# A two-pass matrix MLP with a guarded fallback: moving branch hints, splitting early outputs and shifting one ScalarE square

## Chip, cores, metric

One core of one Trainium2 chip. The metric is the device time of one execution in microseconds (us), as the median of several runs.

In the profiles PE is the tensor engine (PEld its weight loads), DVE is VectorE, ACT is ScalarE, POOL is GpSimd, and SP is the engine that here only issues DMAs. A q behind a name means the engine's sequencer, which runs the waits, jumps and DMA issues. A branch hint is an instruction (BRANCH_PREFETCH_HINT in the traces, 45 to 56 ns), put somewhere ahead of a branch, with which the program tells an engine which way the branch will probably go. Hit and miss are used here for what the traces show at the jump: on SP and DVE the next instruction started 0.45 to 0.54 us after the end of the jump (a hit) or 2.5 to 3.0 us after it (a miss); on PE the branch instruction took 0.4 us, and 3.7 us in the one run without a hint (e6).

## The reference

```python
def reference(x, w1, w2):            # x 16x256x512, w1 512x4096, w2 2048x512, all f32
    h = x @ w1
    gate, value = np.split(h, 2, axis=-1)
    h = np.maximum(gate, 0) * value
    return (h @ w2).astype(np.float32)
```

## The kernel before

The rows of x are worked in four sets of 1024. Each set has a first matmul phase (x by w1, then gate times value into `g`) and a second (g by w2). Both form a 2x2 block product from seven products P1 to P7 (a Strassen-like scheme) in f16. The kernel trusts that only for inputs of a usual size, so along the way it sums squares of x, w1 and w2. In the last set it judges the sums, and a branch at the end runs a slow general body if they don't fit:

```python
    with ExitStack() as fast:
        unfit = fast_way(fast, tc, x2, w1, w2, out2, flag)
    with tc.If(unfit > 0, label="general"):        # line 42 of the kernel
        with ExitStack() as general:
            general_way(general, tc, x2, w1, w2, out2)   # a long body on PE, DVE and SP
```

With the inputs used here the branch always jumps over the general body. The second matmul of a set works on four pairs of row blocks. What each product is followed by (cut):

```python
    class Pair:
        def __init__(self, s, g, t):
            self.end = s == NS - 1 and t == NB // 2 - 1     # only the very last pair: four pieces
        # P2: ScalarE evicts X to o[:,0,:256];  if end: send that piece
        # P3: VectorE evicts W to o[:,0,256:];  send (half or whole row block)
        # P7: VectorE evicts Y to o[:,1,256:];  if end: send that piece
        def P6(self):
            nc.scalar.activation(self.pu[:, 1], self.Y, COPY, scale=1 / GS)   # P7 accumulates into Y after this
            for _ in range(0 if self.s and self.t == 3 else 2 if self.s else 1):
                some_look()                                  # one square of weights, 128x1024, on ScalarE
        def P4(self):
            nc.scalar.activation(self.o[:, 1, :DO // 2], self.Y, COPY, scale=1 / GS)
            self.send(1, slice(0, DO // 2 if self.end else DO))
            if self.t < (2 if self.s else 3):
                some_look()

    ORDER = ("P1 0, P1 1, P2 0, P2 1, P1 2, P5 0, P2 2, P6 0, P3 0, P7 0, P5 1, P6 1, P3 1, P7 1, P4 0, P5 2, P4 1, "
             "P6 2, P3 2, P7 2, P1 3, P4 2, P5 3, P2 3, P6 3, P3 3, P7 3, P4 3")
```

This is the order of sets 1 and 2; sets 0 and 3 use variants of it, which also end with P4 of pair 3. The hints are traced in the last set, but no dependency holds them there. In the built program they come first on PE, DVE and SP, right behind two start-up instructions:

```python
            job(90, lambda: tc.mark_branch_hint_location("general", "LikelyTaken", [ENG.PE, ENG.DVE, ENG.SP]))
```

At the end of set 0, VectorE makes sums of the next set's x, which comes by transposing DMA. The trace has them in the order of the program (the sums from 83.03, the last pair's evictions behind them at 84.36 and 84.70):

```python
            if s == 0:
                sums = sums_of(xo)
                for u in (84, 90):                   # steps of the second matmul's stream
                    job(u, lambda sums=sums: next(sums))
            ...
            advance(stream, 112 - TAIL - 10, jobs)
            if s == 0:
                next(sums)
                next(sums)
```

## Time and profile before

| | before |
|---|---|
| time, median of 3 runs | 311.19 us (311.07 to 311.42) |
| span of the profiled run | 309.16 us, granted clock 0.999 |
| PE busy | 301.5 us, 98% |
| first gap-free PE stretch begins | 23.3 us |
| last ScalarE eviction ends | 304.96 us |
| from there to the end | 4.20 us |

The page's part 1 and part 4 (busy time with its share of the span, and the chain of work that ended last, by engine and by line) say what bounds the kernel:

```profile
PE 301.5 (98%) x1870; PEld 183.2 (59%) x1870; DVE 236.4 (76%) x378; ACT 177.0 (57%) x350; POOL 153.7 (50%) x186
...
PE 93%; DVE 2%; DMA 2%; issue 1%; SPq 0%; ACT 0%; DVEq 0%
PE Y L233 26%; PE X L233 17%; PE W L233 17%; PE Y L333 14%; PE X L333 9%; PE W L333 9%; DMA x_A<-in_x_dram 2%; DVE x_S L164 1%; PE X L448 1%; DVE g L308 1%; PE X L301 1%; PE W L301 1%; PE W L448 0%; PE Y L150 0%; DVE x_S L450 0%
```

PE is the chain (93% of it). I count any wait on PE after 23 us as lost time one for one, and so anything in the tail after PE has finished.

First, a wait on PE in sets 1 and 2. This is the chain in order of time, before, near 223 us (start, length, what, how many):

```profile
222.59 0.87 PE W L333 x8
223.46 0.04 issue
223.50 1.03 PE Y L333 x8
```

Eight matmuls normally take 0.87 us. The group at 223.50 takes 1.03 and comes 0.04 late: 0.20 us lost. The same stands at 150.48. ScalarE's timeline before (start, length, engine, line, operation, shapes) shows what PE waited for:

```profile
221.75 0.38 ACT L376 ACTIVATE o<-Y 128x256 f32<-128x256 f32 x1
222.03 1.05 ACT L179 ACTIVATE sq<-v_B 128x1024 f16<-128x1024 f16 x1
222.98 0.19 ACT L179 ACTIVATION_READ_ACCUMULATOR sq<-v_B 128x1 f32 x1
223.07 0.37 ACT L360 ACTIVATE pu<-Y 128x256 f32<-128x256 f32 x1
223.34 1.06 ACT L179 ACTIVATE sq<-v_T 128x1024 f16<-128x1024 f16 x1
```

The product at 223.50 accumulates into Y, which ScalarE must have read first (`pu<-Y`, 223.07 to 223.44). That read stood behind a square that began at 222.03: 1.04 us from start to start, with its accumulator read in between.

Second, the jump at the end. These are the instructions that the sequencers ran for line 42, the branch, before (engine, operation, count; durations min/median/max in ns; first and last start in us):

```profile
L42 SPq EVENT_SEMAPHORE  x8: 17/17/17, 305.9 to 307.5; - x8
...
L42 PEldq COMPARE_BRANCH  x1: 397/397/397, 303.4 to 303.4; - x1
L42 DVEq COMPARE_BRANCH  x1: 90/90/90, 303.7 to 303.7; - x1
L42 DVEq EVENT_SEMAPHORE  x1: 21/21/21, 304.3 to 304.3; - x1
...
L42 SPq COMPARE_BRANCH  x1: 73/73/73, 305.4 to 305.4; - x1
```

The first instruction after SP's jump starts at 305.9, 0.45 us after the jump ended. SP then waits for eight DMA semaphores, one after the other, until 307.5; the last transfer landed at 307.17. The last ScalarE eviction, from which the tail is counted, was:

```profile
304.58 0.38 ACT L376 ACTIVATE o<-Y 128x256 f32<-128x256 f32 x1 [2.24 <-PE Y L333]
```

The hints stood at the very start:

```profile
L670 SPq BRANCH_PREFETCH_HINT  x1: 56/56/56, 0.7 to 0.7; - x1
L670 DVEq BRANCH_PREFETCH_HINT  x1: 51/51/51, 0.8 to 0.8; - x1
L670 PEldq BRANCH_PREFETCH_HINT  x1: 50/50/50, 0.8 to 0.8; - x1
```

And SP's own waits from 300 us on (engine and line, what it waited for: us in total, times, longest):

```profile
SPq L42 <- SPq L42: 1.7, 3, 0.8
```

That is 1.7 us in three waits: one between the jump and the next instruction (0.45 us), two for landings.

### The profile page before, as it was taken

To read this page: it belongs to the slowest core of one execution; us is meant where nothing else is said; L and a number is where in the kernel's file an instruction comes from. 1 tells how busy PE (TensorE), PEld (TensorE's weight loads), DVE (VectorE), ACT (ScalarE), POOL (GpSimd) and SP (SyncE) were. 2 spreads that over 40 slices of the span, in tenths; PEclk is the share of its full clock that TensorE was granted. 3 is DMA by queue.
4 is the path that set the end of the run, shared out by engine and by line. 5 is a ranking of instruction groups with operands and counts; after the bars stand their busy time and mean duration, and the time that the engine had idled before them with its cause. 6 is when DMAs were issued, how large, how long until landed. Compare 5 with 4: busy or idle time off the path is not lost.

```text
span 309.2 us, 5211 instructions
## 1 busy us (share of the span) xinstructions
PE 301.5 (98%) x1870; PEld 183.2 (59%) x1870; DVE 236.4 (76%) x378; ACT 177.0 (57%) x350; POOL 153.7 (50%) x186
## 2 busy tenths in 40 slices
PE   7999999999999999999999999999999999999994
PEld 3844444588854444478864444458884444448883
DVE  1598888889678888887538888888536888888841
ACT  2588886445865555537855555546956555553231
POOL 2199999930048899500028889700006988700000
PEclk9999999999999999999999999999999999999999
DMA  7977696998594233001354400000325110000132
GB/s 236 355 230 251 176 232 87 196 214 149 164 303 101 69 70 68 2 0 47 127 184 105 119 0 4 0 0 15 122 103 171 37 34 1 0 3 0 70 136 72
DMA packets 37340, 32.87 MB, mean 106 GB/s; under 512 B 14400, under 2 KB 32320, under 8 KB 37184
## 3 DMA queue, kind: packets, MB, share of 16 engines
q1 hardware_dynamic: 31904, 25.70, 27.2%
q0 software_dynamic: 4352, 6.29, 11.8%
q10 hardware_dynamic: 1056, 0.52, 0.6%
q8 instruction: 15, 0.25, 0.3%
q14 instruction: 13, 0.11, 0.1%
HBM read 27.26 MB, written 12.58 MB: 129 GB/s over the span
## 4 chain that ended last, share of the span: by engine, by line
PE 93%; DVE 2%; DMA 2%; issue 1%; SPq 0%; ACT 0%; DVEq 0%
PE Y L233 26%; PE X L233 17%; PE W L233 17%; PE Y L333 14%; PE X L333 9%; PE W L333 9%; DMA x_A<-in_x_dram 2%; DVE x_S L164 1%; PE X L448 1%; DVE g L308 1%; PE X L301 1%; PE W L301 1%; PE W L448 0%; PE Y L150 0%; DVE x_S L450 0%
## 5 line engine op out<-in xcount | busy, mean ns | idle before, releaser
L233 PEld LDWEIGHTS <-w_T 128*128 128x128 f16 x496 | 48.5, 98 | 57.5 <-issue 1.0
L170 POOL TENSOR_TENSOR fold<-xh 128x1024 f32<-128x1024 f16 x16 | 30.3, 1894 | 93.1 <-DMA xh<-x 92.1
L233 PE MATMUL X<-x_A,w_B 128*128 128x512 f16 x248 | 73.7, 379 | 0.2 <-ACT Y L240 0.2
L233 PE MATMUL Y<-x_S,w_T 128*128 128x512 f16 x248 | 73.8, 379 | 0.0
L233 PEld LDWEIGHTS <-w_B 128*128 128x128 f16 x372 | 36.4, 98 | 42.6 <-issue 0.8
L240 ACT COPY Y<-X 128x512 f32<-128x512 f32 x62 | 35.4, 570 | 39.8 <-PE X L233 39.5
L260 DVE SCALAR_TENSOR_TENSOR cc<-W,pu 128x512 f32<-128x512 f32 x62 | 42.8, 691 | 19.5 <-ACT pu L254 19.5
L254 ACT ACTIVATE pu<-Y 128x512 f32<-128x512 f32 x62 | 37.0, 597 | 34.1 <-PE Y L233 32.8
L173 POOL TENSOR_TENSOR fold<-fold 128x512 f32<-128x512 f32 (+2 forms) x96 | 51.8, 540 | 7.5
L333 PEld LDWEIGHTS <-w_stage 128*128 128x128 f16 x512 | 50.0, 98 | 6.3 <-issue 0.4
L266 DVE SCALAR_TENSOR_TENSOR cc<-Y,pu 128x512 f32<-128x512 f32 x62 | 42.8, 691 | 7.2 <-PE Y L233 0.7
L261 DVE SCALAR_TENSOR_TENSOR g<-X,cc 128x512 f16<-128x512 f32 x62 | 42.9, 691 | 2.3
L276 DVE SCALAR_TENSOR_TENSOR g<-Y,cc 128x512 f16<-128x512 f32 x62 | 42.2, 681 | 1.8 <-PE Y L233 1.8
L333 PEld LDWEIGHTS <-g 128*128 128x128 f16 x384 | 37.6, 98 | 8.2
L233 PE MATMUL Y<-x_A,w_T 128*128 128x512 f16 x124 | 36.9, 379 | 0.5 <-DVE cc L266 0.5
L247 ACT ACTIVATE pu<-W 128x512 f32<-128x512 f32 x62 | 37.2, 600 | 0.2 <-ACT Y L240 0.2
L233 PE MATMUL W<-x_S,w_T 128*128 128x512 f16 x124 | 36.9, 379 | 0.0
L233 PE MATMUL W<-x_S,w_B 128*128 128x512 f16 x124 | 36.9, 379 | 0.0
L333 PE MATMUL Y<-v_T,w_stage 128*128 128x256 f16 x256 | 33.2, 272 | 0.1
L333 PE MATMUL X<-v_B,g 128*128 128x256 f16 x256 | 31.9, 273 | 0.0
L164 DVE TENSOR_TENSOR w_stage<-g 128x1024 f16<-128x1024 f16 x32 | 21.5, 686 | 0.2
L365 DVE SCALAR_TENSOR_TENSOR o<-W,pu 128x256 f32<-128x256 f32 x16 | 6.7, 422 | 18.7 <-PE W L333 18.7
(84 smaller groups left out, 283.8 us busy)
## 6 DMA issues: line engine op xcount, KB each, us to landing
out_dram<-o SPq DMA_DIRECT2D x30, 256.0 KB, 2.0
w_stage<-in_w_dram SPq DMA_DIRECT2D x14, 512.0 KB, 5.7
x<-in_x_dram POOLq DMA_DIRECT2D x4, 1024.0 KB, 12.9
xh<-x SPq DMA_DIRECT2D x16, 256.0 KB, 3.1
v_B<-in_w_dram POOLq DMA_DIRECT2D x3, 512.0 KB, 6.3
x_S<-in_x_dram SPq DMA_DIRECT2D x4, 256.0 KB, 5.5
x_A<-in_x_dram SPq DMA_DIRECT2D x3, 256.0 KB, 4.9
w_stage<-in_w_dram ACTq DMA_DIRECT2D x2, 256.0 KB, 4.6
```

What stands on the lines that cost most here:

```text
L164: yield eng.tensor_tensor(o[n], o[i0], o[i1], op=op)
L170: nc.gpsimd.tensor_tensor(fold, t, t, op=MULT)
L173: nc.gpsimd.tensor_tensor(fold[:, :, :m], fold[:, :, :m], fold[:, :, m:2 * m], op=ADD)
L233: nc.tensor.matmul(ps, wop[wn][:, b, self.jb * P:(self.jb + 1) * P], self.xo[xn][:, b, :], start=fresh and b == 0, stop=b == 1, skip_group ...
L240: nc.scalar.copy(out=self.Y, in_=self.X)
L247: nc.scalar.activation(self.p5, self.W, COPY, scale=GS)
L254: nc.scalar.activation(self.u2, self.Y, COPY, scale=GS)
L260: nc.vector.scalar_tensor_tensor(out=self.c12, in0=self.W, scalar=GS, in1=self.u2, op0=MULT, op1=ADD)
L261: nc.vector.scalar_tensor_tensor(out=self.g[:, self.jb, :TH], in0=self.X, scalar=0.0, in1=self.c12, op0=MAX, op1=MULT)
L266: nc.vector.scalar_tensor_tensor(out=self.c22, in0=self.Y, scalar=GS, in1=self.p5, op0=MULT, op1=ADD)
L276: nc.vector.scalar_tensor_tensor(out=self.g[:, self.jb, TH:], in0=self.Y, scalar=0.0, in1=self.c22, op0=MAX, op1=MULT)
L333: nc.tensor.matmul(ps, self.op[an][:, i], vop[wn][:, i], start=name in ("P1", "P5") and i == 0, stop=i == NJ // 2 - 1, skip_group_check=True)
```

## The change

Three edits. The hints are pinned within the last set's second matmul, where they were traced. The outputs of pairs 0 and 1 of the last set go out in four pieces each, like those of pair 3. In sets 1 and 2 the square behind pair 1's P4 goes behind pair 2's P4. Cut to its core:

```diff
-            self.end = s == NS - 1 and t == NB // 2 - 1
+            self.end = s == NS - 1 and t != NB // 2 - 2
...
-            if self.t < (2 if self.s else 3):
+            if self.t in ((0, 2) if self.s else (0, 1, 2)):
                 some_look()
...
+    def hint_here():
+        order.close()
+        traced = nc.cur_bb.bb.instructions
+        n = len(traced)
+        tc.mark_branch_hint_location("general", "LikelyTaken", [ENG.PE, ENG.DVE, ENG.SP])
+        for i in nc.cur_bb.bb.instructions[n:]:
+            last = next(x for x in reversed(traced[:n]) if x.engine == i.engine and "Tile" not in type(x).__name__)
+            tc.add_manual_dep(i, last.name, ...)
+        in_order()
...
-            job(90, lambda: tc.mark_branch_hint_location("general", "LikelyTaken", [ENG.PE, ENG.DVE, ENG.SP]))
+            job(50, hint_here)
```

`hint_here` leaves the fixed order for a moment, traces the hints, ties each to the instruction traced last on its engine, and goes back to the fixed order.

## The prediction

> **What bounds it.** The tensor engine: busy 301.5 us of a 309.2 us span (page, part 1), 93% of the chain that ended last (part 4), at a granted clock of 0.999. From 24 us on it runs nearly without a gap. Reading the start-to-start distances of its matmuls, I find after 24 us only three extra waits worth naming: 0.199 us at 150.48, 0.199 us at 223.50, and about 0.19 us around the counting matmul at 289.86. The rest that is not matmul time is the start (first x tile landing, then VectorE, until 23.3 us) and a tail: the last matmul's ScalarE eviction ends at 304.96, the span at 309.16.

> **The square of weights.** In the middle sets (1 and 2), ScalarE reads one pair's Y (P6 of pair 2) late: in the timeline of ScalarE it runs two squares (about 1.25 us each with the accumulator read) behind two P4 evictions, and the Y read starts at 150.06 and 223.07, 0.44 us before the matmul into that Y that waits for it. The change takes one square from in front of it and puts it behind the next pair's P4, at about 226.7. From the timeline, ScalarE then has 1.24 us of square before the W eviction, whose accumulating matmul starts about 2.2 us later, so no new wait. Worth 2 x 0.20 = 0.40 us, all on the chain.

> **The hints.** Before, they are the first instructions of PE, DVE and SP (56, 51, 50 ns on the sequencers, records of that line). The first x load on SP starts at 0.850; ScalarE's first load, with no hint, at 0.733. Removed: up to 0.11 us on the first x tiles, which head the chain until 6.2 us, part of it lost to shared DMA; I take 0.07. Added: the same three instructions near 290 us. DVE and SP have slack there; PE may lose 0 to 0.1 us, I take 0.03. At the end each hinted engine jumps over the general body. [...] SP resumes 0.45 us after its branch, with a landing until 307.17 to hide in, so I read a hit already before; I expect no gain here. No record shows whether a late hint still works[...].

> **Four pieces.** Pairs 0 and 1 send 8 transfers of 128 KB instead of 4 of 256 KB (the ordered instructions show it), from 282.5 us on. They are long landed at the end; pair 3 is unchanged. But four more transfers rotate the eight DMA semaphores: the last transfer moves from the fourth to the eighth in the order in which SP waits for them. Before, SP gets past the fourth wait at 307.19 and then spends four more waits until 307.53, about 0.07 us each. These now lie before the landing. Worth 0.27 us, on the chain.

> **Sum.** -0.40 - 0.07 + 0.03 - 0.27 = -0.71 us: 311.19 to 310.48 us. I say 310.5, range 310.0 to 311.0. Chance of faster by over 2%: 0.005; within 2%: 0.99; slower: 0.005.

> **What would show it.** Right: no gap on PE near 150.4 and 223.3; first x load at 0.74; after the last landing only one SP wait of that group, span near 308.45. Wrong: a new PE gap near 153 or 226 to 228; PE gap near 290.8; SP resuming over 1 us after its branch.

> **What would make it wrong.** A branch miss at the end[...]; instruction packets at 304.7 to 306.9, which seem to hold the last landing on two DMA engines by 0.4 us, moving earlier or later; the start's gain being swallowed by DMA sharing.

That SP's jump was a hit already before was the reading of the 0.45 us; no run had shown a miss yet. The 0.07 and 0.03 us for the hints are estimates, from the 0.11 us between the two first loads and from the hints' 50 to 56 ns. For the shared DMA the trace before has this: from 3 to 6.5 us, with x and w loads on their way together, the 16 DMA engines were at least 80% busy. How much of the gain that would take, it does not show. That instruction packets hold the last landing is a guess too; measured before, 14 of that transfer's 16 parts had landed by 306.68, the other two at 307.06 and 307.17.

## More of the kernel before

All runs quoted are of the state "fast" unless said otherwise; a program that was run once has the state "unknown".

The chain before near 85 us has no hole:

```profile
83.72 0.90 PE Y L333 x8
84.62 0.43 PE X L233 x2
85.06 0.43 PE W L233 x2
85.49 0.44 PE Y L333 x4
85.92 0.43 PE X L233 x2
```

## The result, and the profile after

| | before | after |
|---|---|---|
| median, same rounds (4 runs each) | 311.31 us (311.07 to 311.74) | 311.70 us (311.15 to 312.04) |
| ratio | | 1.0009, 95% interval 0.9991 to 1.0028 |
| span of the profiled run | 309.16 us | 310.16 us |
| last ScalarE eviction ends | 304.96 us | 304.65 us |
| from there to the end | 4.20 us | 5.50 us |

A ratio is the mean time of one kernel's fast runs over that of the other's fast runs of the same rounds, so it is not quite the ratio of the medians. The change brought nothing that the timing can tell from zero, where 0.7 us less was predicted. The profiled execution of the changed kernel was the slowest of its four (312.04 us), and that of the kernel before (310.94 us) was faster than any of its four, so the spans differ by more than the medians.

The page's part 1, after:

```profile
PE 301.2 (97%) x1870; PEld 183.2 (59%) x1870; DVE 236.4 (76%) x378; ACT 177.2 (57%) x350; POOL 153.7 (50%) x186
```

The line numbers of the changed kernel are 5 higher here (L338 is L333 before). The wait behind the square is gone. The chain after, in order of time, near 223 us:

```profile
222.48 0.87 PE W L338 x8
223.35 0.87 PE Y L338 x8
224.22 0.87 PE X L338 x8
```

ScalarE's timeline after, at the same product:

```profile
222.51 0.38 ACT L365 ACTIVATE pu<-Y 128x256 f32<-128x256 f32 x1 [0.49 <-PE Y L338]
222.79 1.05 ACT L184 ACTIVATE sq<-v_B 128x1024 f16<-128x1024 f16 x1
```

All groups take 0.87 us, and the read of Y starts at 222.51 instead of 223.07. From 86 us to the end of the matmuls PE has no extra wait but the counting matmul's, which is in both kernels.

The jump at the end is what turned. The same instructions of line 42, after:

```profile
L42 SPq EVENT_SEMAPHORE  x8: 17/17/17, 307.9 to 308.5; - x8
...
L42 PEldq COMPARE_BRANCH  x1: 397/397/397, 303.1 to 303.1; - x1
L42 DVEq COMPARE_BRANCH  x1: 90/90/90, 303.4 to 303.4; - x1
...
L42 SPq COMPARE_BRANCH  x1: 73/73/73, 305.1 to 305.1; - x1
L42 DVEq EVENT_SEMAPHORE  x1: 21/21/21, 306.5 to 306.5; - x1
```

SP's own waits from 300 us on, after, are one long one for line 42:

```profile
SPq L42 <- SPq L42: 2.8, 1, 2.8
```

SP jumps at 305.1 and runs its next instruction at 307.9: 2.80 us instead of 0.45. DVE takes 3.04 us instead of 0.54 (jump ends at 303.50, next at 306.55). PE is as before (0.79 us; in both profiles its next instruction starts together with ScalarE's branch). The last transfer landed at 307.23, but SP was not there to see it; it came back at 307.94 and then went through all eight waits. The last eviction, after:

```profile
304.27 0.38 ACT L381 ACTIVATE o<-Y 128x256 f32<-128x256 f32 x1 [2.24 <-PE Y L338]
```

The hints now stand here:

```profile
L687 PEldq BRANCH_PREFETCH_HINT  x1: 45/45/45, 289.7 to 289.7; - x1
L687 DVEq BRANCH_PREFETCH_HINT  x1: 51/51/51, 289.8 to 289.8; - x1
L687 SPq BRANCH_PREFETCH_HINT  x1: 51/51/51, 289.9 to 289.9; - x1
```

And the end of set 0 has a hole. The chain after, in order of time, near 85 us:

```profile
83.43 0.90 PE Y L338 x8
...
84.61 0.15 DVE o L370
84.76 0.18 issue
84.94 0.43 DVE o L375
85.37 0.04 issue
85.41 0.60 PE Y L338 x4
```

VectorE's timeline there, after (in brackets: idle time before, and what ended it):

```profile
83.28 1.42 DVE L169 TENSOR_TENSOR x_S<-x_S,x_A 128x1024 f16<-128x1024 f16 x2 [3.10 <-DMA x_A<-x]
84.61 0.42 DVE L370 SCALAR_TENSOR_TENSOR o<-W,pu 128x256 f32<-128x256 f32 x1
84.94 0.41 DVE L375 SCALAR_TENSOR_TENSOR o<-Y,pu 128x256 f32<-128x256 f32 x1
```

VectorE's two sums wait for transposed x until 83.28 (3.10 us idle, ended by that DMA), and the last pair's evictions stand behind them. PE's P4 of pair 3 needs the second eviction (of Y) and loses 0.37 us. In the profile before, the same sums began at 83.03 and nothing was lost.

The trace's records of instruction packets (queue, start in us) add what the views do not print. Queue 8 moves 16,384 bytes at a time and its number of packets fits PE's stream; queue 14 moves 8,192 bytes at a time and, as I read it, serves the others:

```
from 240 us on, before: q8 246.05 273.09 290.97 304.65            q14 246.60 262.78 273.78 305.19 306.46
from 240 us on, after:  q8 245.64 272.76 290.91 304.32            q14 245.91 262.49 273.61 304.61 306.03 307.13 308.79
```

After the change, queue 14 has two packets more, at the end. Between the hints at 289.8 and 304.61 it has none; by then PE, DVE and ACT have jumped (303.1 to 304.3), and SP jumps 0.45 us later.

All fourteen profiles agree with this. After 300 us, queue 14 has two packets where SP and DVE both hit (the kernel before, e1, e3, e4, e7 with its repeat, e9 with its repeat, e10), three where one of them missed (e5, e8), and four where both missed (the changed kernel, e2, e6). A miss of SP or DVE goes with one more packet of instructions.

### The profile page after: what moved, and what is told of

It reads as the page before. It is cut to its first block, busy times and chain, and to the rows that moved or that the text cites. A ratio compares the mean times of both kernels' runs of the same rounds, so it can differ in the third digit from the quotient of the medians.

```text
span 310.2 us, 5218 instructions
## 1 busy us (share of the span) xinstructions
PE 301.2 (97%) x1870; PEld 183.2 (59%) x1870; DVE 236.4 (76%) x378; ACT 177.2 (57%) x350; POOL 153.7 (50%) x186
## 4 chain that ended last, share of the span: by engine, by line
PE 92%; DVE 3%; DMA 2%; issue 1%; SPq 0%; ACT 0%; DVEq 0%
PE Y L238 26%; PE X L238 17%; PE W L238 17%; PE Y L338 14%; PE X L338 9%; PE W L338 9%; DMA x_A<-in_x_dram 2%; DVE x_S L169 1%; DVE g L313 1%; PE X L306 1%; PE W L306 1%; PE X L453 0%; PE W L453 0%; SPq L449 0%; DVE x_S L455 0%
## 5 line engine op out<-in xcount | busy, mean ns | idle before, releaser
L338 PEld LDWEIGHTS <-w_stage 128*128 128x128 f16 x512 | 50.0, 98 | 5.8
L338 PEld LDWEIGHTS <-g 128*128 128x128 f16 x384 | 37.6, 98 | 8.6 <-issue 0.5
L338 PE MATMUL Y<-v_T,w_stage 128*128 128x256 f16 x256 | 33.2, 273 | 0.0
L338 PE MATMUL X<-v_B,g 128*128 128x256 f16 x256 | 31.9, 273 | 0.0
```

The costliest lines, as they stand in the source:

```text
L338: nc.tensor.matmul(ps, self.op[an][:, i], vop[wn][:, i], start=name in ("P1", "P5") and i == 0, stop=i == NJ // 2 - 1, skip_group_check=True)
```

## The experiments

**Theory A** (a guess when it was made; the runs test only where a hint must stand, not what it does inside). A hint counts only if a packet of instructions for its engine still comes between the hint and the jump. In the changed kernel queue 14 had its last packet ahead of the hints at 273.61, and none between them and DVE's jump. If the one at 304.61 is not SP's either, the late hints of SP and DVE are as good as none; the jump misses, and SP's miss is the new tail. **Rival B.** The extra transfers, or the shifted semaphores, lengthen the tail. **Rival C.** The square moved makes a new wait. Where the expectations below speak of a block of instructions that an engine fetches, what the traces show of it is a packet of instructions, on queue 8 or 14. For the first four runs each edit was done or undone alone. They shared their runs of the kernel before, whose median was 311.34 us; one of those eleven took 314.29 us, which widens all four intervals.

### e1: all edits, hints back at the start

```diff
-            job(50, hint_here)
+            job(90, lambda: tc.mark_branch_hint_location("general", "LikelyTaken", [ENG.PE, ENG.DVE, ENG.SP]))
```

> The changed kernel, but with the three hints first in their streams, as before the change. Theory (the late hints no longer work on SP and DVE; the other two edits pay as predicted): SP resumes about 0.45 us after its branch instead of 2.8 us, DVE 0.5 us instead of 3.0, only one semaphore wait of the branch's end block comes after the last landing, and the time is about 0.67 us under the kernel before: ratio about 0.998. Rival (the tail is longer because of the extra pieces or the moved semaphores, not the hints): SP still resumes over 2 us after its branch, and the time is that of the changed kernel, ratio about 1.001.

Measured: 311.05 us (6 runs, 310.37 to 311.32), ratio 0.998 [0.9949, 1.001]. SP's gap after the jump was 0.455 us, DVE's 0.537, one wait came after the last landing, and eviction's end to span's end took 3.90 us. SP's waits from 300 us on:

```profile
SPq L42 <- SPq L42: 1.3, 3, 0.5
```

The trace is as theory A says, the rival's is not; the timing alone would not settle it.

### e2: the kernel before, hints late

```diff
-            job(90, lambda: tc.mark_branch_hint_location("general", "LikelyTaken", [ENG.PE, ENG.DVE, ENG.SP]))
+            job(50, hint_here)          # with hint_here as in the change
```

> The kernel before, with the hints alone moved late. Theory: SP resumes about 2.8 us after its branch, after the last landing; some 1.0 to 1.2 us slower than before at the end, less up to 0.2 us from the earlier start, so ratio 1.0025 to 1.004. Rival (the hints cost nothing, the pieces do): ratio 0.999 to 1.000.

Measured: 312.64 us (6 runs, 312.12 to 312.94), every run slower than the median of before by 0.78 us or more; ratio 1.003 [0.9999, 1.0061]. The interval just includes 1, because of the outlier before; all six runs lie above ten of those eleven. SP's gap was 2.76 us, DVE's 2.98. SP's waits:

```profile
SPq L42 <- SPq L42: 2.8, 1, 2.8
```

The late hints alone make the loss, without the extra pieces.

### e3: the kernel before, the square moved

```diff
-            if self.t < (2 if self.s else 3):
+            if self.t in ((0, 2) if self.s else (0, 1, 2)):
```

> The kernel before, with only the one square moved in sets 1 and 2. Theory: the two PE gaps of 0.199 us near 150.5 and 223.5 go, no new ones come, 0.40 us faster: ratio 0.9987. Rival (the later square makes a new wait behind pair 2's last product or in the next set): the gaps move to about 153 or 226 to 228 and the ratio is 0.9995 to 1.000.

Measured: 311.01 us (6 runs, 310.77 to 311.76), ratio 0.9981 [0.9949, 1.0012]. Both gaps of 0.199 us are gone and none came behind pair 2. Rival C falls. But this profile had a gap of 0.58 us at 85.83, in set 0, which the edit does not touch: the size of that gap changes from execution to execution, and it can hide the gain in a single look.

### e4: the kernel before, pairs 0 and 1 in pieces

```diff
-            self.end = s == NS - 1 and t == NB // 2 - 1
+            self.end = s == NS - 1 and t != NB // 2 - 2
```

> The kernel before, with only the outputs of pairs 0 and 1 in four pieces. Theory: the last transfer's semaphore becomes the eighth in the order of the final waits, so that one wait and not five comes after the last landing: 0.27 us faster, ratio 0.9991. Rival (more transfers hold the queue or the landings up): the last landing comes later than 2.2 us after its issue and the ratio is 1.000 or more.

Measured: 311.02 us (6 runs, 310.76 to 311.89), ratio 0.9985 [0.9953, 1.0016]. The last landing came 2.17 us after its issue (2.18 before), one wait came after it instead of five, and from that landing to the end took 1.71 us instead of 1.99: 0.28 us, as predicted. Rival B falls.

The next four took theory A apart: which engine's miss counts, and where a hint must stand.

### e5: SP's hint at the start, PE's and DVE's late

```diff
-            job(50, hint_here)
+            job(50, lambda: hint_here([ENG.PE, ENG.DVE]))
+            job(90, lambda: tc.mark_branch_hint_location("general", "LikelyTaken", [ENG.SP]))
```

(`hint_here` now takes the engines as an argument.)

> The changed kernel with SP's hint first in its stream again, the hints of PE and DVE late. Theory: only SP's miss was on the chain; DVE still resumes about 3 us after its branch, near 306.5, before SP needs it, so SP resumes after 0.45 us, one wait follows the last landing, and the time is that of the kernel with all hints at the start: about 311.0, ratio about 0.998. Rival (DVE's late return holds the end up as well): the span ends over 0.5 us later than with all hints at the start.

Measured: 310.64 us (4 runs, 310.36 to 311.21) beside 311.36 before, ratio 0.9977 [0.9959, 0.9996]. DVE still missed (3.02 us, back at 306.38). SP took 0.455 us, and landing to end took 1.71 us, no more than with all hints at the start. Only SP's miss was on the chain.

### e6: no hints

```diff
-            job(50, hint_here)
```

> The changed kernel with no hints at all. Theory (a late hint on SP and DVE is as good as none): SP resumes about 2.8 us after its branch and DVE about 3.0 us, as with the late hints, span about 310.2. [...] PE without one now resumes over 1.5 us after its branch instead of 0.79. Rival (the late hints work in part, the tail's length has another cause): SP's gap grows over 3.5 us.

One look: 312.36 us, span 310.57 (state unknown). SP's gap 2.70 us, DVE's 2.87: as with the late hints. The span is 0.37 us over the 310.2 expected; SP's last DMA issue took 1.08 us instead of 0.33 here, so that its branch came later, and why is open. The new thing is PE, whose branch instruction alone took 3.7 us (0.4 before and after):

```profile
L42 PEldq COMPARE_BRANCH  x1: 3713/3713/3713, 302.9 to 302.9; - x1
```

So PE's late hint did work, and it is the one of the three that still had a packet of instructions to come: hint at 289.7, packet on queue 8 at 290.91 in the changed kernel. Without the hint, queue 8 has two packets after 300 us (303.87 and 307.35) and not one, as in the thirteen other profiles.

### e7: the hints in the first set's second matmul

```diff
+        if s == 0:
+            job(20, hint_here)
...
-            job(50, hint_here)
```

> The changed kernel with the hints in the first set's second matmul, on SP near 82 us. Theory (a hint counts only if its engine still fetches a block of instructions between the hint and the branch): DVE fetches later, near 192 or 274 us, so it resumes after 0.54 us. SP fetches once, near 55 or near 97 us (the packets of instructions do not say of which engine): if at 97, SP resumes after 0.45 us and the time is about 311.0 or less; if at 55, after 2.8 us. Rival (a hint is lost only by being too near to the branch, or by standing anywhere but the start): both hit, or both miss.

Measured: 310.43 us (4 runs, 310.19 to 310.77) beside 311.36 before, ratio 0.9965 [0.9948, 0.9982]. SP's hint ran at 81.68 us, and SP hit (0.455 us); DVE hit too (0.538). Both hit, which the rival also allows; e8 decides. SP's waits from 300 us on:

```profile
SPq L42 <- SPq L42: 1.7, 3, 1.0
```

### e8: the hints in the second set's second matmul

```diff
+        if s == 1:
+            job(20, hint_here)
...
-            job(50, hint_here)
```

> The changed kernel with the hints in the second set's second matmul, near 140 to 155 us. Theory: DVE, which still fetches instructions after that, resumes 0.54 us after its branch; SP, which does not, resumes after 2.8 us, although its hint stands 150 us before the branch. Rival (distance in time decides): both hit.

One look: 311.38 us (state unknown). SP's hint ran at 101.57 us, over 200 us ahead of its branch, and SP missed (2.54 us); DVE's ran at 138.5 and hit (0.536), PE's at 136.0 and was as before. SP's waits:

```profile
SPq L42 <- SPq L42: 2.6, 1, 2.6
```

Between a hint at 81.68 that works and one at 101.57 that does not, queue 14 has one single packet:

```
q14, 30 to 200 us, e7: 36.44 46.98 54.41 97.56 109.69 112.50 186.64 191.54
q14, 30 to 200 us, e8: 36.56 46.71 54.56 97.48 112.25 112.32 186.41 191.60
```

The one at 97.5. The records do not name its engine, but counting does. These are e7's packets on queue 14 from 30 to 300 us, each with the number of traced instructions that an engine had started by then:

```
VectorE   46.98 (66)    109.69 or 112.50 (189 or 194)    191.54 (318)    273.41 (447)
ScalarE   36.44 (59)    109.69 or 112.50 (187 or 192)    186.64 (318)    262.43 (448)
GpSimd    54.41 (61)    246.11 (195)
left      97.56: SP at 81, VectorE at 168, ScalarE at 169, GpSimd at 76
```

The packets of each of the three are 123 to 134 instructions apart (PE's, of twice the bytes, 253 on average), and the one at 97.56 falls between theirs. So it is SP's by elimination, and it lies between SP's instruction 49, where e7's hint stood, and 86, where e8's stood. It is SP's only one between 30 and 300 us: SP runs only some 200 instructions in the whole program. Distance in time does not decide, and neither does the start of the stream.

That the packets differ with where the hints stand shows in one more place. In the nine profiles in which PE and DVE had passed their hints by then, queue 14 has a packet at 109.3 to 110.2 us; in the five others (the changed kernel, e2, e5, e6, e8) it has none there, and two at 112.2 to 112.8. What exactly a hint does inside an engine, no run here shows.

### e9: e7 with a VectorE sum behind the evictions

The hole near 85 us also came and went in these profiles. It is not part of the change, but it swallowed the earlier start. This run puts the second of the two sums after the last pair's evictions:

```diff
-                for u in (84, 90):
+                for u in (84,):
                     job(u, lambda sums=sums: next(sums))
...
             if s == 0:
                 next(sums)
                 next(sums)
+                next(sums)
```

> The changed kernel with the hints in the first set (as in the run before), and at the end of the first set VectorE's second sum of the next set's x placed behind the last pair's two output evictions instead of ahead of them. Theory (the gap of 0.2 to 0.6 us on PE near 85 us, which comes and goes between executions, is pair 3's last product waiting for an eviction of Y that stands behind two sums that wait for transposed x): the gap goes, about 0.3 us faster on average than with the hints in the first set alone: near 310.1 us, ratio to the kernel before about 0.9955. Rival (x itself is late, and PE waits for it anyhow): the gap moves to the product that reads the sum, near 86 us, and the time stays at 310.4.

Measured: 310.20 us (5 runs, 309.99 to 310.86) beside 311.22 before, ratio 0.9967 [0.9953, 0.9981], with no gap on PE.

> The changed kernel with the hints in the first set, again, beside the run with the later sum on the same chip: 310.4 us, ratio about 0.997; SP resumes 0.45 us after its branch.

The kernel of e7 on the same chip: 310.43 us (5 runs, 310.05 to 310.65), ratio 0.9969 [0.9955, 0.9982], with a gap of 0.23 us at 85.36. The two cannot be told apart by these timings; the difference of the medians has the sign and about the size expected. So e9's kernel was run once more:

> The same kernel as in the run with the later sum, again on whatever chip comes. If that order removes the gap near 85 us and not luck, this profile shows no gap over 0.1 us on PE after 24 us, as the first one did, and the time is again near 310.2 us, ratio about 0.9965.

Measured: 310.34 us (6 runs, 309.96 to 310.74) beside 311.58 before, ratio 0.9956 [0.9938, 0.9973]. Again no gap. VectorE's timeline in this profile:

```profile
83.10 0.69 DVE L169 TENSOR_TENSOR x_S<-x_S,x_A 128x1024 f16<-128x1024 f16 x1 [2.93 <-DMA x_A<-x]
83.71 0.42 DVE L370 SCALAR_TENSOR_TENSOR o<-W,pu 128x256 f32<-128x256 f32 x1
84.37 0.43 DVE L375 SCALAR_TENSOR_TENSOR o<-Y,pu 128x256 f32<-128x256 f32 x1 [0.24 <-PE Y L338]
```

x landed about as late as in the profile before (the sum starts at 83.10, against 83.03), but the eviction of Y is now at 84.37 instead of 84.70, and PE's product at 85.20 did not wait. Two looks without a gap do not prove that it never comes back: of the twelve profiles without this edit, four had no gap either (before, e5, e8, e10). The mechanism is visible in the order of the instructions, but that the edit removes the gap is not shown.

### e10: the kernel before, only pair 0 in pieces

```diff
-            self.end = s == NS - 1 and t == NB // 2 - 1
+            self.end = s == NS - 1 and t in (0, NB // 2 - 1)
```

> The kernel before, with only pair 0 (and pair 3 as before) in four pieces: two transfers more instead of four. Theory of the rotating semaphores: the last transfer's semaphore is the sixth in the order of the waits, so three waits (its own and two) come after the last landing, and the time from that landing to the end of the span is 1.85 us, between 1.99 with five and 1.71 with one. Rival (smaller transfers land sooner, or the queue is emptier): the time from landing to end does not follow the count of waits.

One look: 311.31 us (state unknown). Three waits came after the last landing, and from landing to end took 1.84 us. Five, three and one waits gave 1.99, 1.84 and 1.71 us: 0.07 us for each wait. The landing itself was 2.52 us after the issue, later than in e4, so the rival's "sooner landings" are not what counts.

## Why the prediction was wrong, point by point

- **What bounds it:** right. PE's chain, its extra waits and the tail make up the whole difference between the two profiles: -0.40 (squares) -0.28 (start, PE is at its first gap-free stretch at 23.01 instead of 23.30) +0.37 (hole at 85 us) +1.30 (tail) = +0.99 us, and the spans differ by 1.00.
- **The square, -0.40 us:** right, in size and place. Both gaps of 0.199 us went in the profile after and in e3. The timing of e3 alone (ratio 0.9981, interval up to 1.0012) does not tell it from zero.
- **Four pieces, -0.27 us:** right (0.28 in e4), with e10 between. In the changed kernel itself it could not show, because SP came back after the landing and had all eight waits still ahead of it.
- **The hints at the end: this is the step that failed.** "I read a hit already before; I expect no gain here" was right for the kernel before, but the sum then took the late hints as working too, and left a miss to the list of risks ("No record shows whether a late hint still works"). The late hints do not work on SP and DVE. SP's gap went from 0.455 to 2.80 us, and the tail grew by 1.30 us where the prediction had -0.27. Had SP hit, the tail would have ended 1.71 us after the landing at 307.23, at 308.94 instead of 310.16: the miss cost 1.22 us. The evidence for doubting was in the trace before: no packet of instructions followed the hints at 0.8 us until 18.1 us, so no packet need come at once with a hint, and SP ran only 197 instructions in all, beside 501 on VectorE, so that few packets could be its own. I did not count them. That the jump hit before was itself owed to a hint: without any (e6) SP's gap was 2.70 us.
- **The hints at the start, -0.07 us:** mis-sized. In the profiles whose first SP instruction is the hint (before, e1, e3, e4, e5, e10), the stretch begins at 23.24 us on average (23.10 to 23.34); in the eight others at 23.01 (22.91 to 23.10). That is 0.23 us, not 0.07; why it is more than the 0.11 us by which the first load moved is open. In the profile after, the hole near 85 us took it back (+0.37): VectorE's wait for x ended at 83.28 after and 83.03 before. But the hole is no lasting price of the early start. It came in three of the six profiles with SP's hint first (0.18 us on average over the six) and in five of the other six without e9's edit (0.23 us on average).
- **The sum without the miss:** it holds. Squares, pieces and start as measured make -0.40 - 0.28 - 0.23 = -0.91 us, and e7, which has all three and no miss on SP, was 0.93 us below the kernel before by the medians, its repeat 0.79.
- **The hint on PE, +0.03 us:** nothing measurable; the waits around the counting matmul are 0.19 us in both profiles.
- **Late landings at the end:** open. In all profiles with hints, 14 of the last transfer's 16 parts land within 1.70 us of the issue, the last at 2.17 to 2.60. Instruction packets run at that time (before: 304.65, 305.19 and 306.46), and I argued that they are the cause; no run here tells.

The version that came out, e9's, took 310.2 to 310.3 us, 0.3 to 0.4% less than the kernel before in the same rounds, with both intervals clear of 1. The changed kernel (311.70 us) was not run in the same rounds as e9's.
